# An encoder block in FP32 on one core: how the second MLP product opens, exchanges its banks and ends

## The chip, the cores and the metric

The kernel runs on one core of a Trainium2 chip. The metric is the device time of one execution in microseconds, the median of several runs. A core has a matrix engine (TensorE, PE in the profile; PEld is its weight load), a vector engine (VectorE, DVE), a scalar engine (ScalarE, ACT), GpSimd (POOL), and a sync engine (SP) whose queue issues the loads. Matmul results land in PSUM, which holds eight banks of 128 x 512 FP32 values; everything else lies in SBUF.

## The reference

256 tokens of width 2048 go through attention, cross attention to a memory, and an MLP, each with a residual scaled by ALPHA and a layer norm. Only the end concerns the change:

```python
def squared_relu_mlp(h, w_mlp_in, w_mlp_out):
    return jnp.square(jax.nn.relu(h @ w_mlp_in)) @ w_mlp_out      # 2048 -> 8192 -> 2048
...
        x = layer_norm(ALPHA * x + xa, ln2_g[l], ln2_b[l])
        ff = squared_relu_mlp(x, w_mlp_in[l], w_mlp_out[l])
        x = layer_norm(ALPHA * x + ff, ln3_g[l], ln3_b[l])
```

## The kernel before

**Precision.** A product of FP32 matrices is made of three matmuls on split operands. A split (lines 952 to 954, 87 and 88) is two operations: ScalarE copies the source into the shorter type (w_hi), VectorE subtracts that copy from the source (lo). The three matmuls are hi x hi, hi x lo and lo x hi (`mm3`, lines 164 to 166). Weights arrive in blocks of 128 x 2048 (1024 KB) in four buffers (raw_x and three called raw), are split in halves of 1024 columns, and the split parts turn over in four w_hi and four lo buffers. So a split waits until TensorE has read the part four back, and a load waits until its buffer's last reader is done.

**First MLP product.** The hidden matrix has 64 column tiles of 128, in 4 chunks c of 16. The first 8 tiles are made by two hidden groups of four tiles each (`hidden_group`, matmuls at lines 213 and 218, group 0 in acc banks, group 1 in att banks). The other 56 (`hidden_tile`, matmuls at lines 1024 and 1032) stand between the units of the second product. A tile's result is evacuated by ScalarE (line 875) and VectorE (876); two tiles make a pair, and a pair is finished by `stages`: relu and square on ScalarE (888, 889), split into ht (879, 880), sums of its quarters on VectorE (899 to 903), split of the sums into aux (879, 880).

**Second MLP product.** It runs in 8 passes, `PASSES`: chunk c of the hidden matrix by half q of the output's columns, in the order (0,0) (0,1) (1,1) (1,0) (2,0) (2,1) (3,1) (3,0). Passes with the same q that stand next to each other form one run over the same banks; so pass 0 is a run by itself, 1 and 2, 3 and 4, 5 and 6 are runs, and 7 is the last. Each pass has eight units, one for each pair. A P unit multiplies plainly: 24 matmuls of 512 columns. An S unit uses seven products with sums of quarters on both sides: 21 matmuls; the sums of its weights (`push_sums`, line 946) go into s_t. `UNITS` says which is which: most passes open with a P unit, and pass 6 is six S, one P, one S, with a hidden tile before each of its first six units.

**Banks.** Four acc banks xs = x11, x12, x21, x22 take the output's quarters and four att banks pt = p1, p5, p6, p7 the shared products. `res` holds the residual and the running output in SBUF. At the end of a run `close` empties the banks: `swap(i)` brings x11, x12 or x21 into res and `seed` fills the bank with what res holds for the next run's half, so that the next matmuls add to it. At the end of pass 0, where the banks began without a residual, swap is a VectorE operation that scales res and adds the bank (line 1096); at the others it is a ScalarE copy (1084). The merges (1098) then bring p1 and the others from the bank, by way of m_t, into res on VectorE.

**Order.** What goes through `queue` keeps the program's order on its engine. What doesn't (the evacuation of most tiles, the finishing of most pairs) is placed by a planner that reckons with the engines' times. Within the ordered part, `part` (line 956) is the clock: each call splits one part of the weights, counts up by one, and then runs what `after(n, ...)` set down for that count. So n says behind how many further splits something stands; entries of one count keep the order in which they were set down. `banks` and `side` hold work that a split takes along. `finish` takes a pair from `late_finish` when a unit ends or a tile begins.

**LN2 rows.** The multiplication and addition of LN2's gain and bias rows on res (line 1255) is done beside the MLP. The rows of 1024 columns are loaded to all partitions (line 1249) into row_b, half q = 0 first. `side` runs the four operations of q = 0 in hidden group 1, two behind each of the last two splits. Once they are done, the rows of q = 1 are loaded into row_b; their operations stand at counts 6, 8, 10 and 12 in pass 0.

Of the kernel before, what the change touches and what calls it, by code (L numbers as in the profile page):

```python
# [18 lines left out]
P = 128  # L19
# [19 lines left out]
def encoder_kernel(ctx: ExitStack, tc: tile.TileContext, t, out):  # L39
# [965 lines left out]
        todo = [stages(h, c, j0 // 2 + i, queue) for i, h in pairs]  # L1005
        return [lambda i=i, h=h: empty(i, h) for i, h in pairs], todo

    now, late_finish, later, count, held_lo = [], [], [], [0], []

    def after(n, *todo):  # L1010

# [4 lines left out]
    def hidden_tile(it, ps):  # L1016

        _, c, j = it
        for h_ in range(2):
            hi, lo = part(raw_of[it][:, h_ * 1024:(h_ + 1) * 1024])  # L1020
            k0 = 8 * h_

            def w_hi(k):
                queue(nc.tensor.matmul(ps, hi[:, k * P:(k + 1) * P], x2t[:, k0 + k, :],  # L1024
                                       start=k0 + k == 0, stop=k0 + k == KT - 1))

            for k in range(7):
                w_hi(k)
            if h_ == 0:
                w_hi(7)  # L1030
            for k in range(8):
                queue(nc.tensor.matmul(ps[:, 0:S], lo[:, k * P:(k + 1) * P], x2t[:, k0 + k, 0:S],  # L1032
                                       start=False, stop=False))
            if h_ == 1:
                w_hi(7)
        if j % 2 == 0:
            now[:] = [tmp_tile()]
        h = now[0]
        first = c == 0 and LEAD <= j < LEAD + 4
        if first:  # L1040
            after(3 if j == LEAD else 4, lambda: evacuate(ps, h, j % 2, queue))
        else:
            evacuate(ps, h, j % 2)
        if j % 2 and first:
            square, halve, add, halve_sums = stages(h, c, j // 2, queue)
            n = 5
            after(n, square)
            after(n + 2, add, halve)
            after(n + 3, halve_sums)
        elif j % 2:  # L1050
            late_finish.append((h, c, j // 2))

# [2 lines left out]
    def finish():  # L1055

        if late_finish and free["h"] and free["s"]:
            h, c, p = late_finish.pop(0)
            for stage in stages(h, c, p, queue if (c, p) == (NCH - 1, CH // 2 - 1) else free_order):
                stage()  # L1060

    def step():
# [37 lines left out]
    def close(n):  # L1100
# [3 lines left out]
        rs = r11, r12, r21, r22 = quarters(PASSES[n][1])  # L1104

        def swap(i):
            if n == 0:
                merge(rs[i], xs[i], scale=ALPHA)
            else:
                copy(rs[i], xs[i])  # L1110
            seed(n + 1, i)

        if final:
            after(1, lambda: seed(n + 1, 3), lambda: swap(1))
            after(2, lambda: swap(0), lambda: swap(2))
        else:
            after(2, lambda: swap(1), lambda: swap(0))
            after(3, lambda: swap(2))
        if n == 0:
            run["p"] = kept = [row_b[:, i * 512:(i + 1) * 512] for i in range(4)]  # L1120
            copy(kept[0], p1)
# [1 line left out]
            after(5, lambda: copy(kept[2], p6))  # L1123
            return
        copy(m_t, p1)
        after(2, lambda: merge(r11, m_t))
        after(3, lambda: merge(m_t, p6), lambda: merge(r12, m_t, ALU.subtract))
        after(4, lambda: merge(r12, p5), lambda: merge(r22, p5))
        after(5, lambda: merge(m_t, p7, ALU.subtract))
        after(6, lambda: merge(r22, m_t, ALU.subtract))  # L1130
        after(7, lambda: merge(r21, m_t))
        if run["p"]:
# [8 lines left out]
    def one_pass(n):  # L1141
# [6 lines left out]
        if final:  # L1148
            wide = big.tile([P, 8192], F32R, tag="big", name="wide")
            held_lo[:] = [i for i in range(len(sums_h)) if i not in [place["s", c, p] for p in SUMS[c]]]  # L1150
            held_lo.extend(place["s", c, p] for p in SEVENS[PASSES[n - 1]])
        r22 = quarters(q)[3]
        if opens:
            whole = units if final or closes else units + UNITS[n + 1]
            n_s, n_p = whole.count("S"), whole.count("P")
            run["left"] = {id(ps): n_s + 2 * n_p for ps in (x11, x12)}
            run["left"][id(x21)] = run["left"][id(x11)]
            run["left"].update({id(ps): n_s for ps in pt})
            run["seeded"] = {id(ps) for ps in (x11, x12, x21)} if n else set()
            if final:  # L1160
                run["left"][id(x22)] = 2 * n_p
                run["seeded"].add(id(x22))
            run["scale"] = ALPHA if c == 0 else None
            run["s"], run["begun"] = n_s, set()
# [19 lines left out]
        while n_unit < len(units):  # L1184
# [41 lines left out]
            if n % 2:  # L1226
                give("h", c, p)
                if p in SUMS[c]:
                    give("s", c, p)
            finish()  # L1230
        if not final:
            return
        pump(len(banks))
# [10 lines left out]
                mm3(ps, *a(c, k, 1), hi, lo, False, j == len(parts) - 1, queue, True)  # L1244
            queue(stats(sts[1], ps))

    def norm_rows(q):
        for i, w in enumerate("gb"):
            nc.sync.dma_start(row_b[:, i * 1024:(i + 1) * 1024],
                              t[f"ln2_{w}"][q * 1024:(q + 1) * 1024].partition_broadcast(P))  # L1250

    def norm_ops(q):
        o = q * 1024
        return [lambda i=i, b=b, op=op: queue(
            nc.vector.tensor_tensor(out=res[b][:, o:o + 1024], in0=res[b][:, o:o + 1024],
                                    in1=row_b[:, i * 1024:(i + 1) * 1024], op=op))
            for i, op in enumerate((ALU.mult, ALU.add)) for b in range(NB)]

    g3, b3 = s_t, row_b
# [63 lines left out]
    for g in range(LEAD // G):  # L1323
# [2 lines left out]
        wait = [lambda: None]  # L1326

        if g == 0:
            norm_rows(0)
            rows = norm_ops(0)  # L1330
            (a1, a2), (b1, b2, b3_, b4) = first, second
            side.extend(wait * 4 + empty + [a1, b1, a2, b2, b3_, b4] + rows)
            s_in.split, s_in.beside = queued_split, 2
        else:
# [2 lines left out]
            after(2, *empty)  # L1337
            for n, x in ((5, a1), (6, a3), (6, a2), (7, a4), (8, b1), (9, b3_), (9, b2), (11, b4)):
                after(n, x)
            norm_rows(1)  # L1340
    xs, pt = [acc_tile() for _ in range(4)], [att_tile() for _ in range(4)]
    for i, x in enumerate(norm_ops(1)):
        after(2 * i + 6, x)
    for n in range(len(PASSES)):
        one_pass(n)

# [118 lines left out]
```

## Time and profile before

| | |
|---|---|
| median of 3 runs | 1104.6 us (1103.95 to 1104.87) |
| the profiled execution | 1104.91 us, its span 1103.1 us |
| granted TensorE clock, mean | 0.995 |
| VectorE, ScalarE busy | 946.9 us (86%), 672.2 us (61%) |
| hidden group 1 ends, first tile of pass 0 starts | 447 us |
| the first product's last matmul | 1026.5 us |
| pass 7 starts | 1047.9 us |

Times in the rows are microseconds from the span's start. A row of the timeline gives start, time, engine, line, operation, output and inputs, shape and count; in brackets stands how long the engine was idle before it and what ended that. Matmuls are pipelined: each of 512 columns shows about 0.4 us, but the next one starts 0.23 us later, so a stretch's length says more than the busy time. Operations on VectorE and ScalarE overlap by about 0.1 us in the same way.

### The profile page before, as it was taken

To read this page: it belongs to the slowest core of one execution; us is meant where nothing else is said; L and a number is where in the kernel's file an instruction comes from. 1 tells how busy PE (TensorE), PEld (TensorE's weight loads), DVE (VectorE), ACT (ScalarE), POOL (GpSimd) and SP (SyncE) were. 2 spreads that over 40 slices of the span, in tenths; PEclk is the share of its full clock that TensorE was granted. 3 is DMA by queue.
4 is the path that set the end of the run, shared out by engine and by line. 5 is a ranking of instruction groups with operands and counts; after the bars stand their busy time and mean duration, and the time that the engine had idled before them with its cause. 6 is when DMAs were issued, how large, how long until landed. Compare 5 with 4: busy or idle time off the path is not lost.

```text
span 1103.1 us, 15327 instructions
## 1 busy us (share of the span) xinstructions
PE 1079.9 (98%) x5832; PEld 928.1 (84%) x5832; DVE 946.9 (86%) x1310; ACT 672.2 (61%) x992; POOL 36.6 (3%) x43
## 2 busy tenths in 40 slices
PE   9999999999999999989999999999999999999897
PEld 6988899988999878878878888888888878888676
DVE  6878678688889676999989999989999999999786
ACT  6555567546577426656666666666666676676560
POOL 1402000000000000000000000000000000000000
PEclk9999999999999999999999999999999999999999
DMA  9663454466567335646545655665655646556452
GB/s 332 229 230 136 157 195 154 158 224 244 182 209 275 141 110 191 229 153 221 200 155 195 222 196 191 224 216 204 217 197 197 218 164 229 191 193 226 161 183 76
DMA packets 37225, 215.86 MB, mean 196 GB/s; under 512 B 4256, under 2 KB 4896, under 8 KB 13472
## 3 DMA queue, kind: packets, MB, share of 16 engines
q1 hardware_dynamic: 37152, 214.89, 55.1%
q8 instruction: 45, 0.74, 0.3%
q14 instruction: 28, 0.23, 0.1%
HBM read 212.78 MB, written 2.10 MB: 195 GB/s over the span
## 4 chain that ended last, share of the span: by engine, by line
PE 89%; DVE 5%; ACT 2%; DMA 2%; issue 1%; SPq 0%; DVEq 0%; POOL 0%; ACTq 0%
PE acc L1024 16%; PE acc L165 12%; PE acc L166 11%; PE acc L164 11%; PE acc L1032 8%; PE att L165 4%; PE att L166 4%; PE att L164 4%; PE acc L206 2%; PE acc L204 2%; PE acc L205 2%; DVE lo L954 2%; PE acc L213 1%; PE att L213 1%; ACT w_hi L953 1%
## 5 line engine op out<-in xcount | busy, mean ns | idle before, releaser
L1024 PE MATMUL acc<-x2t,w_hi 128*128 128x512 f32 x800 | 207.4, 391 | 0.0
L954 DVE TENSOR_TENSOR lo<-raw,w_hi 128x1024 fp32r<-128x1024 f32 (+1 forms) x182 | 190.8, 1071 | 13.9 <-ACT w_hi L953 13.9
L87 ACT ACTIVATE w_hi<-raw 128x1024 fp32r<-128x1024 f32 (+2 forms) x134 | 131.6, 989 | 109.1 <-PE acc L166 74.0
L88 DVE TENSOR_TENSOR w_lo<-raw,w_hi 128x1024 fp32r<-128x1024 f32 (+2 forms) x130 | 145.9, 1132 | 53.8 <-ACT w_hi L87 52.5
L953 ACT ACTIVATE w_hi<-raw 128x1024 fp32r<-128x1024 f32 (+1 forms) x182 | 165.0, 935 | 18.7 <-PE acc L166 12.0
L1024 PEld LDWEIGHTS acc<-x2t,w_hi 128*128 128x128 f32 x800 | 147.2, 189 | 26.5
L954 DVE TENSOR_TENSOR lo<-s_t,w_hi 128x1024 fp32r<-128x1024 f32 x100 | 121.7, 1220 | 15.1 <-ACT w_hi L953 15.0
L953 ACT ACTIVATE w_hi<-s_t 128x1024 fp32r<-128x1024 f32 x100 | 105.4, 1057 | 41.0 <-DVE lo L954 21.2
L1032 PEld LDWEIGHTS acc<-x2t,lo 128*128 128x128 f32 x800 | 109.1, 190 | 7.8
L1032 PE MATMUL acc<-x2t,lo 128*128 128x256 f32 x800 | 111.6, 282 | 0.0
L875 ACT ACTIVATE tmp<-acc 128x256 f32<-128x256 f32 x54 | 20.4, 384 | 132.5 <-PE acc L1024 128.2
L165 PE MATMUL acc<-lo,ht 128*128 128x512 f32 x180 | 72.3, 402 | 5.8 <-DVE lo L954 5.8
L164 PE MATMUL acc<-w_hi,ht 128*128 128x512 f32 x180 | 71.7, 398 | 3.1 <-ACT w_hi L953 3.0
L954 DVE TENSOR_TENSOR lo<-raw_x,w_hi 128x1024 fp32r<-128x1024 f32 x58 | 70.5, 1218 | 3.3 <-ACT w_hi L953 3.3
L166 PE MATMUL acc<-w_hi,ht 128*128 128x512 f32 x180 | 71.3, 396 | 0.0
L165 PE MATMUL acc<-w_lo,xt 128*128 128x512 f32 (+2 forms) x192 | 69.3, 362 | 0.8 <-DVE w_lo L88 0.8
L946 DVE TENSOR_TENSOR s_t<-s_t,raw 128x512 f32<-128x512 f32 x100 | 68.5, 685 | 0.9
L166 PE MATMUL acc<-w_hi,xt 128*128 128x512 f32 (+2 forms) x192 | 69.2, 361 | 0.0
L164 PE MATMUL acc<-w_hi,xt 128*128 128x512 f32 (+2 forms) x192 | 65.9, 363 | 0.7 <-ACT w_hi L87 0.7
L953 ACT ACTIVATE w_hi<-raw_x 128x1024 fp32r<-128x1024 f32 x58 | 60.6, 1053 | 4.0 <-PE acc L166 2.3
L165 PE MATMUL att<-lo,aux 128*128 128x512 f32 x150 | 58.8, 392 | 2.7 <-DVE lo L954 2.7
L946 DVE TENSOR_TENSOR s_t<-raw 128x1024 f32<-128x1024 f32 x50 | 60.9, 1217 | 0.0
(302 smaller groups left out, 2313.3 us busy)
## 6 DMA issues: line engine op xcount, KB each, us to landing
raw<-in_w_mo SPq DMA_DIRECT2D x62, 1024.0 KB, 4.8
raw_x<-in_w_mc SPq DMA_DIRECT2D x28, 1024.0 KB, 4.8
raw<-in_w_mc SPq DMA_DIRECT2D x28, 1024.0 KB, 4.8
raw<-in_w_out SPq DMA_DIRECT2D x16, 1024.0 KB, 4.8
raw<-in_w_mi SPq DMA_DIRECT2D x8, 1024.0 KB, 4.8
raw<-in_w_b SPq DMA_DIRECT2D x5, 1024.0 KB, 4.9
raw<-in_w_qa SPq DMA_DIRECT2D x16, 256.0 KB, 5.4
raw<-in_w_qa SPq DMA_DIRECT2D x4, 1024.0 KB, 4.9
```

The costliest lines, as they stand in the source:

```text
L87: pin(nc.scalar.activation(hi, src, AF.Copy), pinned)
L88: return pin(nc.vector.tensor_tensor(out=lo, in0=src, in1=f(hi), op=ALU.subtract), pinned)
L164: keep(nc.tensor.matmul(ps, ah, bh, start=start, stop=False, skip_group_check=seeded))
L165: keep(nc.tensor.matmul(ps, ah, bl, start=False, stop=False, skip_group_check=seeded))
L166: keep(nc.tensor.matmul(ps, al, bh, start=False, stop=stop, skip_group_check=seeded))
L204: nc.tensor.matmul(ps, hi, xt[:, k, 0:S], start=k == 0, stop=False)
L205: nc.tensor.matmul(ps, hi, xt[:, k, S:2 * S], start=False, stop=False)
L946: sums.append(lambda: queue(nc.vector.tensor_tensor(out=out, in0=a, in1=b, op=ALU.add)))
L953: queue(nc.scalar.activation(hi, src, AF.Copy))
L954: queue(nc.vector.tensor_tensor(out=lo, in0=src, in1=f(hi), op=ALU.subtract))
L1024: queue(nc.tensor.matmul(ps, hi[:, k * P:(k + 1) * P], x2t[:, k0 + k, :], start=k0 + k == 0, stop=k0 + k == KT - 1))
L1032: queue(nc.tensor.matmul(ps[:, 0:S], lo[:, k * P:(k + 1) * P], x2t[:, k0 + k, 0:S], start=False, stop=False))
```

## The change

Five edits. (1) At the start of pass 0 the banks x11, x12 and x21 are seeded with ALPHA times res, behind the first, second and third split; every swap is then a ScalarE copy. (2) The third exchange, swap(2), stands behind four splits instead of three, that is behind both halves of the next P unit's weights; at the end of pass 6 all three stand behind two splits and only the seed of x22 behind one. (3) In `close` for passes 2, 4 and 6 the merges move: r11 from 2 to 3, the subtraction from r12 from 3 to 4, the addition to r22 from 4 to 5. (4) The last pair (chunk 3, pair 7) is not finished at the end of the sixth unit of pass 6 but behind the two splits of the P unit that follows. (5) The rows of both halves are loaded at once after hidden group 0, q = 0 into row_b and q = 1 into s_t, and all eight operations stand in hidden group 1, four behind each of its last two splits.

```diff
@@ hidden_tile, finish
+        elif (c, j) == (NCH - 1, CH - 1):
+            last_pair.append((h, c, j // 2))
         elif j % 2:
             late_finish.append((h, c, j // 2))
...
-            for stage in stages(h, c, p, queue if (c, p) == (NCH - 1, CH // 2 - 1) else free_order):
+            for stage in stages(h, c, p):
                 stage()
@@ close
         def swap(i):
-            if n == 0:
-                merge(rs[i], xs[i], scale=ALPHA)
-            else:
-                copy(rs[i], xs[i])
+            copy(rs[i], xs[i])
             seed(n + 1, i)
 
         if final:
-            after(1, lambda: seed(n + 1, 3), lambda: swap(1))
-            after(2, lambda: swap(0), lambda: swap(2))
+            after(1, lambda: seed(n + 1, 3))
+            after(2, lambda: swap(1), lambda: swap(0), lambda: swap(2))
         else:
             after(2, lambda: swap(1), lambda: swap(0))
-            after(3, lambda: swap(2))
+            after(4, lambda: swap(2))
...
         copy(m_t, p1)
-        after(2, lambda: merge(r11, m_t))
-        after(3, lambda: merge(m_t, p6), lambda: merge(r12, m_t, ALU.subtract))
-        after(4, lambda: merge(r12, p5), lambda: merge(r22, p5))
-        after(5, lambda: merge(m_t, p7, ALU.subtract))
+        after(3, lambda: merge(r11, m_t), lambda: merge(m_t, p6))
+        after(4, lambda: merge(r12, m_t, ALU.subtract), lambda: merge(r12, p5))
+        after(5, lambda: merge(r22, p5), lambda: merge(m_t, p7, ALU.subtract))
         after(6, lambda: merge(r22, m_t, ALU.subtract))
@@ one_pass
+        if n == 0:
+            for i in range(3):
+                after(i + 1, lambda i=i: seed(0, i))
...
-            run["seeded"] = {id(ps) for ps in (x11, x12, x21)} if n else set()
+            run["seeded"] = {id(ps) for ps in (x11, x12, x21)}
...
             finish()
+            if last_pair and not late_finish:
+                square, halve, add, halve_sums = stages(*last_pair.pop(), queue)
+                after(2, square, halve, add, halve_sums)
@@ norm rows, hidden groups
-    def norm_rows(q):
-        for i, w in enumerate("gb"):
-            nc.sync.dma_start(row_b[:, i * 1024:(i + 1) * 1024],
-                              t[f"ln2_{w}"][q * 1024:(q + 1) * 1024].partition_broadcast(P))
+    def norm_rows():
+        for q, rows in enumerate((row_b, s_t)):
+            for i, w in enumerate("gb"):
+                nc.sync.dma_start(rows[:, i * 1024:(i + 1) * 1024],
+                                  t[f"ln2_{w}"][q * 1024:(q + 1) * 1024].partition_broadcast(P))
...
-                                    in1=row_b[:, i * 1024:(i + 1) * 1024], op=op))
+                                    in1=(row_b, s_t)[q][:, i * 1024:(i + 1) * 1024], op=op))
...
-            norm_rows(0)
-            rows = norm_ops(0)
+            norm_rows()
+            ops = norm_ops(0) + norm_ops(1)
+            rows = [lambda i=i: [x() for x in ops[i:i + 2]] for i in range(0, 8, 2)]
...
-            norm_rows(1)
...
-    for i, x in enumerate(norm_ops(1)):
-        after(2 * i + 6, x)
```

More of the change, by code (lines that the diff above doesn't have):

```diff
@@ L1006, in hidden_group @@
         return [lambda i=i, h=h: empty(i, h) for i, h in pairs], todo
-    now, late_finish, later, count, held_lo = [], [], [], [0], []
+    now, last_pair, late_finish, later, count, held_lo = [], [], [], [], [0], []
     def after(n, *todo):
```

## The prediction

> **What bounds the kernel now.** I read the page first.
>
> ```profile
> span 1103.1 us, 15327 instructions
> ...
> PE 1079.9 (98%) x5832; PEld 928.1 (84%) x5832; DVE 946.9 (86%) x1310; ACT 672.2 (61%) x992; POOL 36.6 (3%) x43
> ...
> raw<-in_w_mo SPq DMA_DIRECT2D x62, 1024.0 KB, 4.8
> ```
>
> TensorE carries the span, and the change touches no matmul, so it can only move TensorE's waits. 98% hides them: a matmul that waits, or runs at a lower clock, partly counts as busy. So I cut the trace into stretches that each hold one unit's matmuls: 24 for a plain (P) unit, 21 for a seven-product (S) unit. Columns: stretch, length, busy time and count of TensorE, weight load, VectorE, ScalarE, GpSimd, then clock, DMA share, GB/s.
>
> ```profile
> 734.00:739.47 5.47, 5.47 (x26) 4.51 (x25) 2.68 (x4) 4.44 (x7) 0.00 (x0) 1.00 0.93 356
> 551.69:561.33 9.64, 7.64 (x25) 5.59 (x24) 7.76 (x12) 6.15 (x10) 0.00 (x0) 0.82 0.40 120
> ...
> 1031.53:1043.11 11.58, 7.72 (x25) 5.59 (x25) 8.11 (x10) 4.42 (x6) 0.00 (x0) 0.85 0.39 117
> 1047.87:1054.61 6.74, 5.91 (x25) 4.32 (x24) 4.39 (x6) 5.33 (x8) 0.00 (x0) 1.00 0.72 280
> 541.34:546.12 4.78, 4.78 (x22) 3.94 (x21) 4.05 (x5) 4.55 (x7) 0.00 (x0) 1.00 0.70 262
> 474.80:481.63 6.83, 5.09 (x22) 3.87 (x21) 6.83 (x10) 4.93 (x8) 0.00 (x0) 1.00 0.44 154
> 487.20:494.39 7.19, 5.37 (x22) 3.79 (x21) 6.54 (x10) 5.87 (x7) 0.00 (x0) 1.00 0.54 196
> 902.62:907.75 5.13, 4.96 (x21) 3.37 (x20) 5.13 (x7) 5.00 (x7) 0.00 (x0) 1.00 0.61 208
> ```
>
> The first row is a P unit without a wait, 5.47 us (0.228 a matmul); the fifth an S unit without one, 4.78. Against these, the P unit that opens pass 1 loses 4.17, the P unit inside pass 6 loses 6.11, the first unit of pass 7 loses 1.27, and the first two S units of pass 0 lose 2.05 and 2.41. Where the clock stands at 0.82 and 0.85, part of the loss is slow matmuls after the wait. These five places are nearly all that can be won: 16.0 us.
>
> **Part 1: norm rows at once.** Eight VectorE operations on 1024 columns multiply and add the LN2 rows. Four run at the end of hidden group 1 and four between the splits of pass 0; now all eight stand in group 1, four behind the seventh split and four behind the eighth.
>
> ```profile
> L1255 DVE TENSOR_TENSOR res<-res,row_b x8: 1215/1218/1220, 439.7 to 475.6; 128x1024 f32<-128x1024 f32 x8
> ```
> ```profile
> 439.74 2.35 DVE L1255 TENSOR_TENSOR res<-res,row_b 128x1024 f32<-128x1024 f32 x2
> 442.01 1.22 DVE L954 TENSOR_TENSOR lo<-raw,w_hi 128x1024 fp32r<-128x1024 f32 x1
> 443.14 2.36 DVE L1255 TENSOR_TENSOR res<-res,row_b 128x1024 f32<-128x1024 f32 x2
> 445.42 2.35 DVE L954 TENSOR_TENSOR lo<-raw_x,w_hi 128x1024 fp32r<-128x1024 f32 x2
> ...
> 487.81 0.42 DVE L876 TENSOR_TENSOR tmp<-acc,tmp 128x256 f32<-128x256 f32 x1 [1.07 <-ACT tmp L875]
> ```
> ```profile
> 445.14 1.12 PE L218 MATMUL att<-x2t,lo 128*128 128x256 f32 x8
> ...
> 448.85 1.12 PE L1032 MATMUL acc<-x2t,lo 128*128 128x256 f32 x8
> ...
> 478.99 0.50 PE L165 MATMUL att<-lo,aux 128*128 128x512 f32 x1 [1.74 <-DVE lo L954]
> ```
>
> Two operations hold VectorE for 442.01 - 439.74 = 2.27 us. With two more ahead of it the eighth lo starts at 444.28 and ends at 445.50; its matmuls want it at 445.14: about 0.42 lost. The first tile's lo moves from 445.42 by 4.54 to 449.96 and ends at 451.18; its matmuls want it at 448.85, or 449.27 after the first loss: 1.97 more. What follows is ready in time (the next lo's end at 454.8 and 455.9 and are wanted after 456.8), so TensorE runs 2.39 us late from there. In return four operations, 4.54 us of VectorE, vanish between the splits before the first S unit. Walked on by VectorE's order (1.14 us for a 1024-wide operation, 0.60 for 512, 1.0 for the three that form a pair's sums, 0.35 for an evacuation): at 457.0 it has left the first half of the P unit behind it, at 464.1 the tiles in front of the S unit but one; there it stands until 466.6, for a w_hi buffer that TensorE, 2.39 us late, frees; then come four lo's, four operations of 512 for two pairs, their sums, three weight sums and an evacuation, to 477.75. The S unit's first lo of weight sums ends at 478.98; the matmul wants it at 479.47, so the 2.05 (1.74 of it idle before 478.99) are gone. The second S unit waits on VectorE standing for 1.07 us at the evacuation of 487.81, which waits for TensorE; four operations fewer do not change that order, and VectorE reaches it at the same time as before. It is an unqueued operation that the planner places: placed later, the unit would lose about 0.5 instead of 2.41. I keep the place. Sum: 2.39 - 2.05 = **+0.35**, between -1.6 (evacuation later) and +2.4 (neither wait shrinks).
>
> The four row loads now follow each other ahead of raw_x on SP's queue.
>
> ```profile
> 402.82 0.42 SPq L935 DMA_DIRECT2D raw_x<-in_w_mc  x1
> 412.95 9.71 SPq L152 DMA_DIRECT2D raw<-in_w_mi  x3
> ```
> ```profile
> 418.68 2.00 ACT L953 ACTIVATE w_hi<-raw 128x1024 fp32r<-128x1024 f32 x2
> ...
> 446.53 1.22 ACT L875 ACTIVATE tmp<-att 128x256 f32<-128x256 f32 x4 [4.27 <-PE att L213]
> ```
>
> At 4.8 us per 1024 KB, the extra megabyte puts the end of this burst at 402.8 + 14.4 = 417.2 at worst, so the block issued at 412.95 and split at 418.68 could land some 4 us late. Group 1's first matmuls then wait 0.5 at most; I take 0.
>
> **Part 2: seeded from the first run on.** Three ScalarE copies (seeds) are added at the start of pass 0, 0.60 us each by the rows below. ScalarE idles 4.27 us before 446.53, and two hidden tiles' matmuls come before these banks are used: 0; uncovered, 1.8. At the end of pass 0 three VectorE merges become ScalarE copies, and the third exchange moves from between the two halves of the next P unit's weights to behind them.
>
> ```profile
> 553.79 0.50 PE L164 MATMUL acc<-w_hi,ht 128*128 128x512 f32 x1 [1.24 <-ACT w_hi L953]
> 555.05 0.50 PE L165 MATMUL acc<-lo,ht 128*128 128x512 f32 x1 [0.76 <-DVE lo L954]
> ```
> ```profile
> 547.34 1.20 ACT L1084 ACTIVATE acc<-res 128x512 f32<-128x512 f32 x2 [0.90 <-DVE res L1096]
> 548.47 1.04 ACT L953 ACTIVATE w_hi<-raw 128x1024 fp32r<-128x1024 f32 x1
> ...
> 552.17 0.60 ACT L1084 ACTIVATE acc<-res 128x512 f32<-128x512 f32 x1
> 552.69 1.04 ACT L953 ACTIVATE w_hi<-raw 128x1024 fp32r<-128x1024 f32 x1
> ```
> ```profile
> 546.62 1.28 DVE L1096 SCALAR_TENSOR_TENSOR res<-res,acc 128x512 f32<-128x512 f32 x2
> ...
> 550.69 0.68 DVE L1096 SCALAR_TENSOR_TENSOR res<-res,acc 128x512 f32<-128x512 f32 x1
> ...
> 553.77 1.22 DVE L954 TENSOR_TENSOR lo<-raw,w_hi 128x1024 fp32r<-128x1024 f32 x1 [0.51 <-ACT w_hi L953]
> ```
>
> TensorE waits for the second half's w_hi (1.24 us idle) and then its lo (0.76). That w_hi stands behind the third seed, which stands behind the third merge. After, ScalarE does four copies (2.4 us) from about 545.2, with a pair's two activations of 1.2 among them, so the first w_hi starts near 548.7, as now; the second follows at 549.7, three microseconds earlier. Its lo ends by 552.2 and is wanted at 551.69 + 4 x 0.228 = 552.6. The third exchange ends near 552, its bank is wanted at 555.8. All **-4.17** goes. If the planner leaves the tile's evacuation ahead of that lo, as it stood, the lo ends at 551.7 (the tile's end) + 0.4 + 0.42 + 1.22 = 553.8 and 1.2 comes back: -4.17 to -3.0.
>
> **Part 3: later exchange and merges in the other passes.**
>
> ```profile
> 720.84 0.68 DVE L1098 TENSOR_TENSOR m_t<-m_t,att 128x512 f32<-128x512 f32 x1
> ...
> 722.50 1.22 DVE L954 TENSOR_TENSOR lo<-raw,w_hi 128x1024 fp32r<-128x1024 f32 x1
> ...
> 885.49 0.69 DVE L1098 TENSOR_TENSOR res<-res,m_t 128x512 f32<-128x512 f32 x1 [0.60 <-ACT res L1084]
> ```
>
> Between the two lo's at 720 stand two merges and one more operation; after, the first merge (now at 885.49, in idle time) is one of those two and another leaves: still two, about -0.1 at each of two places. But in pass 5 that merge moves from idle time into a stretch in which VectorE is full up to the S unit of 902.62: its wait grows by 0.6 less 0.13. Sum -0.2 + 0.47 = **+0.3**, from -0.5 to +1.2.
>
> **Part 4: the last pair two splits later.**
>
> ```profile
> 1028.18 0.62 ACT L888 ACTIVATE tmp<-tmp 128x512 f32<-128x512 f32 x1
> ...
> 1031.88 0.63 ACT L879 ACTIVATE aux<-tmp 128x512 fp32r<-128x512 f32 x1 [1.75 <-DVE tmp L903]
> 1032.41 3.46 ACT L953 ACTIVATE w_hi<-raw 128x1024 fp32r<-128x1024 f32 x4
> ```
> ```profile
> 1028.31 1.22 DVE L954 TENSOR_TENSOR lo<-s_t,w_hi 128x1024 fp32r<-128x1024 f32 x1 [0.52 <-ACT w_hi L953]
> ```
>
> The P unit of pass 6 wants its weights at 1031.53; their w_hi stands at 1032.41, behind the pair's chain. After, both w_hi run from 1028.2 to 1030.3, the lo's end at 1030.6 and (a weight sum between) 1032.95; the second is wanted at 1032.44, so 0.55 is lost instead of 6.11. The chain, 5.05 us by its rows (1028.18 to 1033.2), starts at 1030.3, waits for the second lo and ends at 1035.85, inside the P unit. Behind it come two weight sums (1.3) and the next S unit's first lo, which ends at 1038.38 where 1037.78 is wanted: 0.6, and 0.3 at its third. Sum -5.56 + 0.9 = **-4.67**; if the whole chain showed in that S unit it would be -1, if none, -6.1.
>
> In pass 7 the first unit's second half no longer stands behind an exchange: 1.27 becomes 0.07. The three exchanges then end at 1045.7, the second unit's first lo at 1047.85, and two merges (1.2) still precede its second lo: ready 1050.3, wanted 1049.64, 0.65 lost against 0.1 now. Sum **-0.65**.
>
> Sum: 0.35 - 4.17 + 0.3 - 4.67 - 0.65 = -8.8 us. The profiled execution took 1104.91 (span 1103.1 and 1.8 around it), which makes 1096.1; it stands 0.3 above the median of 1104.6, so I predict **1095.8**.
>
> The clock shows itself at 0.82 in the row of 551.69, after two waits of 1.24 and 0.76 us with one matmul between, and at 1.00 in that of 474.80 with one wait of 1.74. The Trainium skill (TensorE: Matmul & The Clock Gate, "What's actually happening") says the clock halves after an idle window of about 3.4 us; the trace differs: two waits of 2.0 us together were enough. By that page my new waits of 0.42 and 1.97 would leave the clock up, and the sum would stand.
>
> **Rivals.**
> A. The early wait trips the clock. In the row of 551.69, 4.17 less the waits of 1.24 and 0.76 leaves 2.2 for slow matmuls; paid again at 449, 1098.0. For it: two new waits within 6 us. Against: the 1.00 in the rows of 474.80 and 487.20.
> B. One wait is only exchanged: the chain of the last pair shows in the following S unit, or the evacuation keeps ahead of the lo in pass 1: 1095.8 + 3.7 or + 1.2, 1099.5 or 1097.0. For it: VectorE has no room between 1029.5 and 1040 by my walk.
> C. Slower: the planner lays the unqueued evacuations anew, ahead of the S units' lo's, as it stands at 487.81. That costs 7.19 - 4.78 = 2.4 a unit; from four units on it eats the gain. Six units: 1110. Against: the S unit of 541.34 shows 4.78, and little around these operations moves.
> D. It does not do what it says: the waits are set by something else that ends as late, and the time stays at 1104.6. Against: the rows of 552.69 and 1032.41 start right behind the operations that move.
>
> **Chances.** Forecast 0.62 (own range 1093.5 to 1098.5, from the bounds of parts 1, 2 and 4), A 0.10, B 0.14, C 0.09, D 0.05. Faster by over 0.2% (2.2 us, about what a measurement tells from nothing): 0.86; within it 0.05; slower 0.09. The range, 1092.5 to 1101, reaches over A and B.
>
> **What would show it.** In the trace after: the P units that open pass 1 and stand in pass 6 take about 5.5 and 6.0 at clock 1.00; the S unit behind the latter 5.7; TensorE waits near 445.5 and 449.3 by 0.4 and 2.0; the first S unit of pass 0 takes 4.8 and the second about 7. It is wrong if either P unit keeps more than 2 us of wait, or S units elsewhere lose theirs.

## The result and the profile after

The changed kernel took 1094.56 us, the median of five runs (1094.45 to 1094.79); the kernel before, beside it, took 1104.87 (1103.95 to 1105.63). The ratio is 0.9907, with a 95% interval from 0.9893 to 0.9922. The prediction was 1095.8, within 1092.5 to 1101.0.

The page of the kernel after: its span, then the busy time of each engine.

```profile
span 1092.8 us, 15329 instructions
...
PE 1074.3 (98%) x5832; PEld 925.1 (85%) x5832; DVE 944.1 (86%) x1307; ACT 675.5 (62%) x998; POOL 36.6 (3%) x43
```

Three VectorE operations went (1310 to 1307) and six ScalarE copies came (992 to 998): the merges and seeds of edit 1. TensorE's share is 98% in both, so again only the stretches say anything. Here they are for the kernel after, with the columns of the prediction: the first matmuls of hidden group 0, the end of group 1, the first tile, the first two S units of pass 0, the P units of passes 1, 3 and 6, the S unit behind the last of these, and the first two units of pass 7.

```profile
397.85:400.70 2.85, 2.85 (x16) 2.51 (x17) 2.58 (x6) 1.01 (x2) 0.00 (x0) 1.00 0.00 0
440.81:445.53 4.72, 4.47 (x26) 3.60 (x25) 4.72 (x5) 2.08 (x4) 0.00 (x0) 1.00 0.17 33
445.53:453.08 7.55, 5.83 (x33) 4.83 (x32) 7.55 (x11) 5.96 (x10) 0.00 (x0) 1.00 0.52 182
475.28:480.06 4.78, 4.78 (x22) 3.94 (x21) 4.78 (x7) 4.06 (x7) 0.00 (x0) 1.00 0.66 219
485.63:492.79 7.16, 5.33 (x23) 3.79 (x21) 6.51 (x10) 5.85 (x7) 0.00 (x0) 1.00 0.51 187
550.09:555.55 5.46, 5.46 (x26) 4.51 (x24) 4.72 (x8) 4.28 (x8) 0.00 (x0) 1.00 0.54 194
716.31:722.40 6.09, 5.78 (x25) 4.43 (x24) 6.09 (x11) 2.73 (x5) 0.00 (x0) 1.00 0.50 174
1026.14:1032.29 6.15, 5.75 (x25) 4.43 (x24) 5.35 (x10) 3.21 (x5) 0.00 (x0) 1.00 0.49 171
1032.29:1038.02 5.73, 5.36 (x22) 3.79 (x21) 5.73 (x7) 5.60 (x8) 0.00 (x0) 1.00 0.48 167
1038.02:1043.50 5.48, 5.48 (x25) 4.46 (x24) 2.65 (x4) 4.78 (x8) 0.00 (x0) 1.00 0.97 390
1043.50:1049.96 6.46, 5.75 (x25) 4.43 (x24) 6.42 (x9) 2.01 (x3) 0.00 (x0) 1.00 0.49 172
```

The same view of the kernel before, for stretches that the prediction did not show: the first matmuls of hidden group 0, the S unit behind the P unit of pass 6, and the first two units of pass 7, each with its 24 matmuls (the prediction's row of 1047.87 ends 0.15 before the unit does).

```profile
398.32:402.76 4.44, 4.44 (x17) 3.79 (x18) 3.27 (x7) 1.01 (x2) 0.00 (x0) 0.62 0.00 0
...
1043.11:1047.87 4.76, 4.76 (x22) 3.94 (x21) 3.58 (x3) 4.73 (x8) 0.00 (x0) 1.00 0.55 203
1047.87:1054.76 6.89, 6.06 (x26) 4.43 (x24) 4.54 (x6) 5.48 (x8) 0.00 (x0) 1.00 0.70 273
1054.76:1060.44 5.68, 5.68 (x26) 4.43 (x24) 5.60 (x7) 2.01 (x3) 0.00 (x0) 1.00 0.53 185
```

The P unit of pass 1 went from 9.64 to 5.46 and that of pass 6 from 11.58 to 6.15, both at clock 1.00. The first S unit of pass 0 went from 6.83 to 4.78. The S unit behind pass 6's P unit pays 0.97 of this back. And a stretch that the change does not touch, hidden group 0, takes 2.85 instead of 4.44: its clock stood at 0.62 before.

The time between the two traces can be followed by the start of the same matmul in both, after minus before, at the borders of the parts. The profiled executions differ by 10.29 us (1104.91 to 1094.62).

| stretch | offset at its start, end | difference | predicted |
|---|---|---|---|
| up to the first new wait, at the end of hidden group 1 | 0, -2.00 | -2.00 | 0 |
| part 1, to the end of pass 0's S units | -2.00, -1.60 | +0.40 | +0.35 |
| part 2, P unit of pass 1 | -1.60, -5.78 | -4.18 | -4.17 |
| part 3, passes 2 to 6 | -5.78, -5.39 | +0.39 | +0.3 |
| part 4, P unit of pass 6 and the S unit behind it | -5.39, -9.85 | -4.46 | -4.67 |
| pass 7 | -9.85, -10.48 | -0.63 | -0.65 |

The rest of the span gives 0.2 back. The five parts make -8.48 where the prediction's sum was -8.8. The forecast was 1.2 too high because of the first row: without its 2.00 this execution would have come out near 1096.6, above the forecast. Of the 2.00, 1.58 is group 0's clock (the rows of 397.85 and 398.32, with the same matmuls) and 0.45 lies in the first 43 us, where the weights arrive.

**How part 1 looks.** VectorE's timeline of the kernel after, at the end of hidden group 1: four norm rows, a lo, four norm rows, and then the first tile's lo's.

```profile
437.74 4.62 DVE L1260 TENSOR_TENSOR res<-res,row_b 128x1024 f32<-128x1024 f32 x4
442.28 1.22 DVE L954 TENSOR_TENSOR lo<-raw,w_hi 128x1024 fp32r<-128x1024 f32 x1
443.42 4.63 DVE L1260 TENSOR_TENSOR res<-res,s_t 128x1024 f32<-128x1024 f32 x4
447.96 2.35 DVE L954 TENSOR_TENSOR lo<-raw_x,w_hi 128x1024 fp32r<-128x1024 f32 x2
```

TensorE's timeline in the same place: the two matmul groups that wait, the idle time in brackets.

```profile
443.55 1.21 PE L218 MATMUL att<-x2t,lo 128*128 128x256 f32 x8 [0.25 <-DVE lo L954]
...
449.23 0.98 PE L1032 MATMUL acc<-x2t,lo 128*128 128x256 f32 x6 [1.72 <-DVE lo L954]
```

Behind the four operations of 443.42 the first tile's lo ends at 449.18, and its matmuls start at 449.23. Measured by the start of the waiting matmul, the two waits cost 0.41 and 1.89 us; the matmul behind each wait takes 0.1 longer, which makes 0.50 and 1.98. The prediction had 0.42 and 1.97.

**How part 4 looks.** ScalarE's timeline of the kernel after, then VectorE's, the first ahead of the P unit of pass 6, the second in it.

```profile
1022.94 2.01 ACT L953 ACTIVATE w_hi<-raw 128x1024 fp32r<-128x1024 f32 x2
1024.86 0.61 ACT L888 ACTIVATE tmp<-tmp 128x512 f32<-128x512 f32 x1
```
```profile
1029.84 0.69 DVE L880 TENSOR_TENSOR aux<-tmp,aux 128x512 fp32r<-128x512 f32 x1 [0.70 <-ACT aux L879]
1030.45 1.41 DVE L946 TENSOR_TENSOR s_t<-s_t,raw 128x512 f32<-128x512 f32 x2
1031.78 1.22 DVE L954 TENSOR_TENSOR lo<-raw,w_hi 128x1024 fp32r<-128x1024 f32 x1
```

Both w_hi are now ahead of the pair's square (1022.94 against 1024.86), so the unit's weights no longer stand behind the chain. The chain ends at 1030.53 in the middle of the P unit; two halves of a weight sum follow, and the next S unit's first lo ends at 1033.0, where TensorE had stood for a moment: this is the larger part of the 0.97.

### The profile page after: what moved, and what is told of

Same layout as the page of the kernel before. It is cut to its first block, busy times and chain, and to the rows that moved or that the text cites. A ratio compares the mean times of both kernels' runs of the same rounds, so it can differ in the third digit from the quotient of the medians.

```text
span 1092.8 us, 15329 instructions
## 1 busy us (share of the span) xinstructions
PE 1074.3 (98%) x5832; PEld 925.1 (85%) x5832; DVE 944.1 (86%) x1307; ACT 675.5 (62%) x998; POOL 36.6 (3%) x43
## 4 chain that ended last, share of the span: by engine, by line
PE 91%; DVE 5%; ACT 2%; issue 1%; DMA 1%; SPq 0%; DVEq 0%; POOL 0%; ACTq 0%
PE acc L1024 16%; PE acc L165 12%; PE acc L164 12%; PE acc L166 12%; PE acc L1032 9%; PE att L165 4%; PE att L166 4%; PE att L164 4%; PE acc L206 2%; PE acc L204 2%; PE acc L205 2%; DVE lo L954 2%; PE acc L213 1%; PE att L1024 1%; ACT w_hi L953 1%
## 5 line engine op out<-in xcount | busy, mean ns | idle before, releaser
L164 PE MATMUL acc<-w_hi,ht 128*128 128x512 f32 x180 | 70.2, 390 | 0.0
L166 PE MATMUL acc<-w_hi,ht 128*128 128x512 f32 x180 | 70.1, 389 | 0.0
```

The lines of the kernel that those rows point to most:

```text
L164: keep(nc.tensor.matmul(ps, ah, bh, start=start, stop=False, skip_group_check=seeded))
L166: keep(nc.tensor.matmul(ps, al, bh, start=False, stop=stop, skip_group_check=seeded))
```

## The experiments

Four questions were open. Does each wait go for the reason given (parts 2 and 4)? What are the small terms of parts 1 and 3 worth? Where do the 2.0 us at the start come from? And can the waits that are left be had too? The kernels ran in three series; the kernel before, run beside each, had medians of 1104.3, 1104.8 and 1105.6. Ratios are to it, so a change against the kernel after is read by comparing ratios (0.9907) and by the stretches of the traces. The lengths that have no row below are the stretches of the same matmuls in that kernel's trace.

**The norm rows as before (part 1 undone).**

```diff
-            norm_rows()
-            ops = norm_ops(0) + norm_ops(1)
-            rows = [lambda i=i: [x() for x in ops[i:i + 2]] for i in range(0, 8, 2)]
+            norm_rows(0)
+            rows = norm_ops(0)
...
+            norm_rows(1)
+    for i, x in enumerate(norm_ops(1)):
+        after(2 * i + 6, x)
```

> The changed kernel with the norm rows as they were: q = 0 in hidden group 1, q = 1 loaded behind it and worked off at counts 6 to 12. My walk: the changed kernel's two waits at the end of group 1 (0.41 and 1.88 us) go, and the first S unit of pass 0 waits for its lo again (about 1.8); 0.4 us faster than the changed kernel's 1094.6, so 1094.2. Rival: the 1.8 us that the changed kernel's trace gains before hidden group 1 (the first matmuls of group 0 at clock 1.00 instead of 0.55 to 0.60) come with the earlier row loads; then they are lost here, 1095.6 or more, and the matmuls of group 0 start slow again.

It took 1094.44 us (1093.38 to 1097.29), ratio 0.9914 [0.9898, 0.9931]. The stretches of this kernel: the first tile and the first S unit of pass 0.

```profile
444.78:450.35 5.57, 5.57 (x34) 4.92 (x33) 5.19 (x8) 5.54 (x10) 0.00 (x0) 1.00 0.92 344
472.55:479.41 6.86, 5.12 (x23) 3.87 (x21) 6.86 (x10) 4.97 (x9) 0.00 (x0) 1.00 0.43 153
```

The tile takes 5.57 instead of 7.55 and the S unit 6.86 instead of 4.78: the wait is moved and not removed, as worked out. Behind the S unit this trace stands 0.66 ahead of the kernel after, 0.2 of it from the start; so part 1 costs some 0.4 to 0.5 us, which the times do not resolve. Group 0's first matmuls take 2.86 us in this trace too, with the old rows, so part 1 is not what sped it up.

**The last pair as before (part 4 undone).**

```diff
-        elif (c, j) == (NCH - 1, CH - 1):
-            last_pair.append((h, c, j // 2))
...
-            for stage in stages(h, c, p):
+            for stage in stages(h, c, p, queue if (c, p) == (NCH - 1, CH // 2 - 1) else free_order):
...
-            if last_pair and not late_finish:
-                square, halve, add, halve_sums = stages(*last_pair.pop(), queue)
-                after(2, square, halve, add, halve_sums)
```

> The changed kernel with the last pair finished at the end of the sixth unit of pass 6, as before. My walk: the P unit of pass 6 takes 11.6 us again instead of 6.0 and the S unit behind it 4.8 instead of 5.7, 4.6 us slower than the changed kernel: 1099.2. Rival (the wait is only exchanged, the pair's chain being paid in the next S unit anyway): less than 2 us slower, up to 1096.6.

It took 1101.36 us (1099.95 to 1103.22), ratio 0.9977 [0.9964, 0.9989]. The P unit of pass 6:

```profile
1026.28:1039.24 12.96, 9.07 (x25) 6.58 (x25) 8.11 (x10) 4.43 (x6) 0.00 (x0) 0.74 0.45 154
```

The wait is back and the S unit behind it is whole again (4.77), so the deferral makes this gain. In this trace the unit is 12.96 long, not the 11.58 of the kernel before: the clock is at 0.74 and not 0.85, that is, more matmuls after the waits ran slowly. By the two units, part 4 is worth 4.46 us against the kernel before and 5.85 against this one. The whole trace is 6.7 longer than that of the kernel after (1099.5 against 1092.8), more than the 4.6 expected: besides the clock, the first two units of pass 7 take 5.67 and 6.92 here, 0.65 more than in the kernel after, and no run shows why.

**The first run not seeded, its exchange by VectorE merges (half of part 2).**

```diff
         def swap(i):
-            copy(rs[i], xs[i])
+            if n == 0:
+                merge(rs[i], xs[i], scale=ALPHA)
+            else:
+                copy(rs[i], xs[i])
...
-        if n == 0:
-            for i in range(3):
-                after(i + 1, lambda i=i: seed(0, i))
```

> The changed kernel without the seeds of the first run: at the end of pass 0 the three banks are merged on VectorE with the scale, as before; the third exchange stays behind both weight halves. If the place of the third exchange is what counts, the second w_hi of the P unit that opens pass 1 no longer stands behind a merge, and the unit stays near 5.5 us: 1094.6 to 1095.1. Rival: the merges on VectorE are what holds the weights up; the unit falls back to 9.6: 1098.8.

**The third exchange behind three splits again, the seeds kept (the other half).**

```diff
-            after(4, lambda: swap(2))
+            after(3, lambda: swap(2))
```

> The changed kernel with the third exchange behind three splits again (between the halves of the next P unit's weights) at the ends of passes 0, 2 and 4; the seeds of the first run stay. By the walk the copy and the seed put 1.15 us ahead of the second w_hi; in pass 1 its lo is ready about 0.1 us after it is wanted, in passes 3 and 5 VectorE's merges end later anyway: 1094.6 to 1095.0, so either half of the edit alone would do. Rival: the place of the exchange is what counts, the P unit that opens pass 1 falls back to 9.6: 1098.8; or the P units of passes 3 and 5 lose 1 each.

**Both halves undone.** The two edits above together.

> The changed kernel with both halves of the edit at the ends of passes 0, 2 and 4 undone: no seeds in the first run (VectorE merges with the scale) and the third exchange behind three splits. Each half alone kept the P unit that opens pass 1 near 5.5 us. If the wait needs both (the merge on VectorE ahead of the third seed, and that seed ahead of the second w_hi), it comes back here: the P unit takes 8 to 9.6 us, 1098 to 1099. Rival: the wait was removed by something else that moved (the planner's place for the evacuation, say); the unit stays at 5.5 to 6 and the time near 1095.5.

Without the seeds the time was 1094.91 us (1094.56 to 1095.57), ratio 0.9915 [0.9901, 0.9930]; with the early exchange 1095.53 (1094.74 to 1096.93), 0.9922 [0.9907, 0.9937]; with both undone 1099.76 (1099.3 to 1101.13), 0.9959 [0.9945, 0.9974]. The P unit of pass 1 in the first of these kernels:

```profile
550.39:555.86 5.47, 5.47 (x26) 4.42 (x24) 4.01 (x9) 5.01 (x9) 0.00 (x0) 1.00 0.51 192
```

In the second:

```profile
550.24:555.87 5.63, 5.63 (x25) 4.43 (x24) 5.43 (x8) 4.29 (x8) 0.00 (x0) 1.00 0.56 188
```

In the third, group 0 and the P unit of pass 1:

```profile
398.31:402.74 4.43, 4.43 (x16) 3.82 (x17) 3.28 (x7) 1.01 (x2) 0.00 (x0) 0.61 0.00 0
552.10:561.63 9.53, 7.53 (x25) 5.54 (x24) 7.45 (x11) 6.14 (x10) 0.00 (x0) 0.82 0.37 119
```

The wait needs both: a third exchange between the two halves of the weights, and a VectorE merge ahead of its seed. Either half of part 2 takes it away (5.47 and 5.63 against 9.53); the two gains do not add. The late exchange is worth another 0.3 in each of the P units of passes 3 and 5 (6.38 against 6.09 and 6.39 against 6.09); behind the latter, shorter waits give 0.2 of it back. For the time, the late exchange would have done without the seeds.

The third trace also has group 0 at the low clock, though that kernel is the changed one in everything ahead of pass 0. So this clock is not a matter of the change.

**The kernel before, once more,** unedited, for one profile.

> The kernel before, once more, for its trace. In its first trace the first matmuls of hidden group 0 (398 to 402) ran at clock 0.55 to 0.60 and cost some 1.4 us; in five traces of kernels with the change they ran at 1.00. If that is the clock's phase and not the change, it can be either way here: a trace with clock 1.00 there and a span near 1101.7 shows it. If the slow matmuls stand there again with a span near 1103, the change (or what it does to the program ahead of that place) stays a suspect.

**The changed kernel, once more,** unedited.

> The changed kernel once more, timed on the same chip as the three beside it: 1094.6 within 1 us, since its traces so far show no stretch at a lower clock behind a wait. If the clock trips in some executions here as it does in those of the kernel before, single times up to 1097.

The kernel before took 1100.86 us in this one execution, 6.2 more than the profiled execution of the kernel after. Group 0 and the P units of passes 1 and 6:

```profile
397.06:399.93 2.87, 2.87 (x16) 2.53 (x17) 2.60 (x6) 1.02 (x2) 0.00 (x0) 1.00 0.00 0
548.89:556.90 8.01, 6.02 (x25) 4.43 (x24) 6.17 (x9) 6.15 (x10) 0.00 (x0) 1.00 0.38 131
1027.08:1039.03 11.95, 8.75 (x26) 6.21 (x25) 8.11 (x10) 4.42 (x6) 0.00 (x0) 0.71 0.39 130
```

The changed kernel took 1096.05 (1095.71 to 1096.31), ratio 0.9919 [0.9901, 0.9936]. Its group 0:

```profile
398.04:402.45 4.41, 4.41 (x16) 3.81 (x17) 3.27 (x7) 1.01 (x2) 0.00 (x0) 0.62 0.00 0
```

Each of the two kernels has been seen with group 0 at clock 1.00 and at 0.62. So most of the first row of the table of offsets is this, worth about 1.55 (4.41 - 2.86), and no part of the change. Its other part need not be the change either: the two traces of the kernel before differ by 1.26 in the first 60 us, more than the 0.45 there. The P unit of pass 1 shows the same: 9.64 at clock 0.82 in one execution and 8.01 at 1.00 in another, behind the same two waits of 1.24 and 0.76; pass 6's unit took 11.58 at 0.85 and here 11.95 at 0.71. So the wait that part 2 removes is worth 2.55 (8.01 - 5.46) by itself and 4.18 when the clock falls behind it. One pair of executions can show the change as 10.3 us (1104.91 against 1094.62) or as 6.2; by medians, the two series that have both kernels show 10.3 and 9.6.

**The first merge behind two splits again in the runs that are not last (a piece of part 3).**

```diff
-        after(3, lambda: merge(r11, m_t), lambda: merge(m_t, p6))
+        after(2, lambda: merge(r11, m_t)) if not final else after(3, lambda: merge(r11, m_t))
+        after(3, lambda: merge(m_t, p6))
```

> The changed kernel with the merge of m_t into r11 behind two splits again at the ends of passes 2 and 4 (behind three, as changed, at the end of pass 6). By the prediction's part 3 the merge then runs in VectorE's idle time: the waits of the P units that open passes 3 and 5 (0.48 each) shrink by 0.5 each, and the waits in pass 5 up to its first S unit (0.40 and 0.63) shrink by 0.6 together: 1093.0 to 1093.6. Rival: the second lo is set by ScalarE, not by the merges: no change, 1094.6.

It took 1093.76 us (1093.35 to 1094.15), ratio 0.9902 [0.9886, 0.9919]. The P units of passes 3 and 5 and the S unit behind the latter's tile:

```profile
716.16:721.62 5.46, 5.46 (x25) 4.51 (x24) 5.46 (x10) 3.10 (x6) 0.00 (x0) 1.00 0.55 194
...
883.07:888.56 5.49, 5.49 (x25) 4.34 (x24) 5.49 (x11) 2.34 (x4) 0.00 (x0) 1.00 0.55 191
894.23:900.35 6.12, 5.46 (x23) 3.71 (x21) 6.12 (x8) 4.88 (x7) 0.00 (x0) 1.00 0.55 199
```

Both P units are without a wait (they lost 0.6 each in the kernel after), and the wait of 0.4 behind pass 5's, for a bank that a VectorE merge empties, is gone as well. In the kernel after this last wait stood in TensorE's timeline:

```profile
890.34 0.94 PE L1024 MATMUL acc<-x2t,w_hi 128*128 128x512 f32 x3 [0.24 <-DVE res L1100]
```

The S unit takes 6.12 instead of 5.92: 0.2 of the gain is lost there again, and the wait for that unit's first lo did not shrink as expected.

The span of this trace is 1.5 shorter than that of the kernel after (1091.3 against 1092.8); the times of the two executions differ by 0.7 (1093.92 against 1094.62). This is the fastest version that was run, though its ratio and the changed kernel's lie within each other's intervals.

**Two more evacuations in program order.** Aimed at the second S unit of pass 0, where VectorE stands at an evacuation placed by the planner.

```diff
-        first = c == 0 and LEAD <= j < LEAD + 4
+        first = c == 0 and LEAD <= j < LEAD + 6
```

> The changed kernel with the evacuation of the next two tiles of pass 0 (c = 0, j = 12 and 13) queued four splits later instead of left to the planner, and their pair finished in the queue as the pairs before. My reading of the wait in the second S unit of pass 0 (2.1 us at 487 and 489): VectorE stands before the planner's evacuation until TensorE ends the tile. Then the unit takes about 5.3 instead of 7.2 us: 1092.7 to 1093. Rival: VectorE is simply full there; the wait stays within 0.5: 1094.2 to 1094.6.

It took 1096.65 us (1095.96 to 1097.11), ratio 0.9929 [0.9914, 0.9943]. The second S unit, and then TensorE's timeline two S units later:

```profile
486.24:491.84 5.60, 5.07 (x22) 3.86 (x21) 5.60 (x8) 5.58 (x7) 0.00 (x0) 1.00 0.65 234
```
```profile
510.58 0.50 PE L165 MATMUL acc<-lo,ht 128*128 128x512 f32 x1 [1.06 <-DVE lo L954]
...
512.32 0.50 PE L165 MATMUL att<-lo,aux 128*128 128x512 f32 x1 [0.77 <-DVE lo L954]
```

The unit gained 1.56 (1.9 was expected), and the two waits came back, with the same lengths, two S units later, at the first evacuation that the planner still places. The wait was moved.

**The norm rows spread over all of group 1's splits.**

```diff
-            side.extend(wait * 4 + empty + [a1, b1, a2, b2, b3_, b4] + rows)
+            side.extend(wait * 3 + [run_ops(0, 3)] + empty + [a1, lambda: (b1(), run_ops(3, 2)()), a2, b2]
+                        + [lambda: (b3_(), run_ops(5, 1)()), b4, run_ops(6, 1), wait[0], run_ops(7, 1), wait[0]])
```

(`run_ops(i, n)` runs n of the eight operations from the i-th on.)

> The changed kernel with the eight norm row operations spread over hidden group 1 where VectorE idles in the trace of before (3.3 us before 427.3, 2.1 before 432.4, 0.7 before 437.7): three behind the second split, two behind the fourth, one each behind the sixth, seventh and eighth, instead of four and four at the end. If the two waits at the end of group 1 (0.41 and 1.88 us) come only from the place of these operations, they go and nothing comes in their stead: 2.3 us faster than the changed kernel. Rival: the evacuation of group 0 and the pairs of group 1 are late instead and TensorE waits there: less than 1 us gained, or slower.

It took 1095.76 us (1093.14 to 1096.21), ratio 0.9911 [0.9891, 0.9932]. Its first tile and its second S unit, and under them TensorE's two waits in that S unit:

```profile
447.49:453.06 5.57, 5.57 (x33) 4.92 (x32) 4.46 (x7) 5.54 (x10) 0.00 (x0) 1.00 0.44 175
...
485.61:494.38 8.77, 6.95 (x22) 4.92 (x21) 8.12 (x11) 5.86 (x7) 0.00 (x0) 0.81 0.40 149
```
```profile
488.43 0.50 PE L165 MATMUL acc<-lo,ht 128*128 128x512 f32 x1 [1.05 <-DVE lo L954]
490.17 0.72 PE L165 MATMUL att<-lo,aux 128*128 128x512 f32 x1 [0.76 <-DVE lo L954]
```

The same two matmuls in the kernel after:

```profile
488.45 0.50 PE L165 MATMUL acc<-lo,ht 128*128 128x512 f32 x1 [1.05 <-DVE lo L954]
490.19 0.50 PE L165 MATMUL att<-lo,aux 128*128 128x512 f32 x1 [0.78 <-DVE lo L954]
```

The 2.5 us of new waits at group 1's end are gone, and 0.7 came in their place inside group 1, where a split stands behind the row operations. So up to the second S unit this trace stands 1.73 ahead of the changed kernel's in the same series. But the clock fell in that unit, behind waits as long as those of the kernel after, and it took 8.77 instead of 7.16: at the end 0.1 is left. The gain is in the waits, and an execution can show it or not: the four of this kernel took 1093.14 at a mean clock of 0.999, and 1095.61 to 1096.21 at 0.995 and 0.996.

**The third weight sum behind the S unit's first split.** Aimed at the 0.97 behind part 4 and at the wait ahead of the first S unit of pass 5. `part` takes a sum along behind its split, so the sum that is left when the unit begins now stands behind the unit's first split.

```diff
-                while sums:
-                    sums.popleft()()
-                for src, todo in (...):
+                for i, (src, todo) in enumerate((...)):
+                    while i == 2 and sums:
+                        sums.popleft()()
```

> The changed kernel with the last weight sum of an S unit put behind the split of the unit's first part instead of ahead of it. The S unit behind the P unit of pass 6 waits 0.53 us for its first lo, the first S unit of pass 5 0.63; both stand behind that sum (0.66 us on VectorE). If VectorE's order there is what the last pair's chain costs, both waits go: 0.8 to 1.2 us faster than the changed kernel. Rival: the wait only moves to the unit's third lo: within 0.3.

It took 1097.73 us (1096.4 to 1098.06), ratio 0.9932 [0.9914, 0.9950], against 1096.05 of the changed kernel in the same series. Its second S unit of pass 0, and the S unit behind pass 6's P unit:

```profile
486.13:493.91 7.78, 5.36 (x22) 3.79 (x21) 7.13 (x11) 5.87 (x7) 0.00 (x0) 1.00 0.44 158
...
1033.63:1039.25 5.62, 5.35 (x23) 3.78 (x21) 5.54 (x8) 4.91 (x7) 0.00 (x0) 1.00 0.48 175
```

It brought 0.1 and 0.2 where it was aimed (5.73 to 5.62, and 5.93 to 5.72 in the first S unit of pass 5) and cost 0.6 in the second S unit of pass 0, 0.3 and 0.2 at the P units of passes 3 and 5, and 0.2 and 0.4 in the first two units of pass 7. In the second S unit the sum now stands right ahead of the second lo, for which TensorE waits 1.66 us instead of 1.05: a sum taken from one lo's way is put into another's.

**Three of these edits in one kernel:** the rows spread, the third weight sum later, the first merge early.

> The changed kernel with the rows spread, the sum later, and the first merge behind two splits again at the ends of passes 2 and 4: 2.3 + 0.9 + 1.5 us if the three are independent, since they stand in different stretches: 4.7 us faster than the changed kernel, 1089.9, and faster than both kernels. If one takes another's gain back, 2 to 4 us.

It took 1094.66 us (1092.84 to 1096.51), ratio 0.9910 [0.9884, 0.9936]. Its second S unit:

```profile
483.10:492.48 9.38, 6.96 (x22) 4.93 (x21) 8.73 (x12) 5.86 (x7) 0.00 (x0) 0.82 0.39 132
```

The P unit of pass 3 has lost its wait (5.50), the one of pass 5 the greater part (5.84 against 6.49, with the wait for the bank), and the first tile takes 5.57, so the single gains are there. The second S unit gives back 2.2 against the kernel after, 0.6 of it as with the sum alone and the rest with the clock at 0.82. The sum of gains was not reached, and by its times this kernel can't be told from the changed one.

## Why the prediction was right, step by step

**Part 1** (+0.35): +0.40, right in sign, size and place. The waits of 0.42 and 1.97 were 0.50 and 1.98, the first S unit took 4.78, and the second kept its 7.16, as the choice to "keep the place" of the planner's evacuation had it. Undoing the part took the first tile's wait away and brought the S unit's back.

**Part 2** (-4.17): -4.18. The chain given for it (third merge, third seed, second w_hi, its lo) is shown by undoing its halves. What the prediction did not see is that either half was enough. And the 4.17 was no fixed price: 2.55 of it is wait, 1.63 a fall of the clock that comes in some executions only. That the size is met to 0.01 is luck in so far: against the second trace of the kernel before it would be 2.55.

**Part 3** (+0.3): +0.39, by misses that cancel. The P unit of pass 3 gained 0.25 (6.34 to 6.09) and not 0.1; that of pass 5, expected to gain 0.1, lost 0.17 and the tile behind it 0.11; the S unit took 5.92 instead of 5.52, 0.40 where 0.47 was reckoned (the prediction's row of 902.62 leaves out the unit's first 0.85 us). The piece named as the cost, the first merge moved out of VectorE's idle time, was shown by moving it back: from the P unit of pass 5 to the end of that S unit 0.8 came back. But the merge was priced only there. Moved back it also freed the P unit of pass 3 of 0.6, a loss that the prediction, reckoning with "still two" operations between the two lo's, took for given.

**Part 4** (-4.67): -4.46. The 0.55 left in the P unit was 0.68 (6.15 less 5.47), the 0.9 behind it 0.97. The wait was not exchanged, so rival B falls here: undone, 5.85 us come back in the two units, the slower clock included. In pass 1 its other form, the evacuation ahead of the lo, falls with the unit's 5.46.

**Pass 7** (-0.65): -0.63, again by two misses that cancel. The first unit gained 1.41 (6.89 to 5.48) where 1.20 was reckoned from a row that ends too early, the second lost 0.78 (5.68 to 6.46) where 0.55 was.

**The row loads** were taken at 0; no wait for them shows at the start of group 1.

**The base.** The 1.2 us that are missing come from here: the sum was made against one execution whose group 0 ran at clock 0.62, and no step asked whether that slow stretch would stand in every execution. How near the forecast comes is thus in part the luck of the execution. In the kernel after's profiled execution (1094.62, its five runs lie within 0.4) the clock stood at 1.00; in that of the changed kernel's second series (1096.31) it fell, and that series' median of 1096.05 is met within 0.3.

**Rival A**, the clock falling at the new early waits near 449, is in none of the nine traces that have them (the kernel after and eight others). Its mechanism exists: the clock fell in the second S unit of pass 0, behind old waits, when the rows were spread. Its price was put at 2.2, what the waits of 1.24 and 0.76 leave of 4.17; the fall alone cost 1.63 (9.64 less 8.01). **Rival C** did not come: but for the S unit behind pass 6's P unit (0.97 longer) and the first of pass 5 (0.40), the S units kept their lengths or gained. **Rival D** falls with the two P units.

## What to carry to other kernels

Where one engine carries the span, cut its trace into stretches of equal work and hold each against one that has no wait; the difference, and not the busy share, is what a change of order can win. What another engine has to finish should stand behind all of the next unit's weights and not between their halves; when a full engine lies behind the wait, moving one operation out of the way of one wait puts it in the way of the next, as with the weight sum and the evacuations. And a short wait has two prices, its own length and the chance of a slower clock behind it, so a trace of one execution gives either 2.5 us or 4.2 for the same wait.

## What the runs showed of the hardware that was not expected

The granted clock after a wait is not settled by the length of the wait. TensorE's timeline at the start of group 0, in the kernel before and then in the kernel after:

```profile
398.32 1.97 PE L213 MATMUL acc<-x2t,wide 128*128 128x512 f32 x4 [1.57 <-ACT x2t L757]
```
```profile
397.85 1.16 PE L213 MATMUL acc<-x2t,wide 128*128 128x512 f32 x4 [1.57 <-ACT x2t L757]
```

The idle time ahead of these matmuls is the same, and they take 1.97 or 1.16. The clock of this stretch fell in the kernel before, in two of the edited kernels and in the changed kernel's second series, and stayed at 1.00 in the other traces, the kernel before's second among them; the price is 1.55 us. In the second S unit, waits of 1.05 and 0.76 to 0.78 us left the clock at 1.00 in the kernel after and at 0.81 with the rows spread, and there the matmul at 490.17 took 0.72 instead of 0.50. The Trainium skill (TensorE: Matmul & The Clock Gate, "What's actually happening") has the clock fall after an idle window of about 3.4 us and says that the window runs freely, so that the point of change varies. The second part would fit what is seen here, though no run tested it; the first does not, since the two waits in the S unit make 1.81 us together and the clock fell.

The copy that fills a bank costs hardly more than the one that empties it. ScalarE's timeline of the kernel after, at the end of pass 0: a copy out of a bank and a seed.

```profile
543.54 0.60 ACT L1086 ACTIVATE res<-acc 128x512 f32<-128x512 f32 x1
...
549.11 0.60 ACT L1086 ACTIVATE acc<-res 128x512 f32<-128x512 f32 x1
```

In this trace the 16 copies from res into a bank take 0.61 on the mean, the 12 from a bank into res 0.59. So a VectorE merge of 0.68 was given for ScalarE copies of 0.6, on the engine that is busy for 62% of the span and not 86%.
